# Maximum products of an attention stage in pairs of 64 rows

## The chip, the cores and the metric

The kernel runs on one core of a Trainium2 chip. The time is device time in microseconds (us) from start to end of one execution; the median of several executions counts. Names of the engines as in the profile: PE is TensorE's matmul stream, PEld its weight loads, DVE is VectorE, ACT is ScalarE, POOL is GpSimd, SP issues the DMAs.

## The reference, cut to what matters

One layer of an encoder: 2048 positions, width 1024, float32. Attention has 8 query heads of width 64 on 2 key heads, then comes a gated MLP on chunks, an output projection and a feed-forward part with a convolution. The change lies in the attention alone:

```python
q = rmsnorm(q.reshape(B, S, N_Q_HEADS, HEAD_DIM), g_q[l])
k = rmsnorm(k.reshape(B, S, N_KV_HEADS, HEAD_DIM), g_k[l])
q = apply_axial_rope(q, cos, sin)
k = apply_axial_rope(k, cos, sin)
...
s = jnp.einsum('bqkgd,bskd->bkgqs', qi, k, preferred_element_type=jnp.float32) * scale
p = jax.nn.softmax(s, axis=-1)
return jnp.einsum('bkgqs,bskd->bqkgd', p.astype(v.dtype), v)
```

## The kernel before, in words

Every float32 factor of a matmul is split into a high part and a low part of a narrower type (`h` and `l`), and products are summed from high by high, high by low and low by high. The stages are: projections, attention with the output projection of the block of queries before, the up-projection and the down-projection.

The attention stage works in 32 units: 4 blocks `b` of 512 queries times 8 query heads `hq`. Unit `n` uses these tiles. `K1[i]` holds for key head `i` the 64 rows of the keys' high parts above the 64 rows of their low parts. `K2[i]` holds the high parts again on rows 0 to 63, and a row of -1 on row 64. `X1[n]` holds the queries' high parts twice, on rows 0 to 63 and on rows 64 to 127. `X2[n]` holds the queries' low parts and, on row 64, the maximum of each query's scores. A score tile `st` of 128 keys by 512 queries is the matmul of `K1` with `X1` (L618) plus that of `K2` with `X2` (L619), so the maximum is subtracted by the second matmul. ScalarE then takes the exponential twice (L625 rounded into `ph`, L626 in place), VectorE forms the low part `pl` (L627), and TensorE multiplies `ph` (L607) and `pl` (L613) with the values.

The maximum of unit `n` is found ahead of its scores, by `max_piece`: 16 products per unit, each of 128 queries by 512 keys, with the queries as weights (L538). Each product is reduced by VectorE into a column of `mx` (L539). `max_finish` reduces the columns, transposes them on TensorE (L547) and sends the row to `X2` by DMA. The loop over a unit's 16 key tiles `kt` calls one step of `attend` and one `max_piece`, six steps ahead of the unit that uses it. Scores and products take their PSUM banks from one pool, `ps_s`, with four buffers. Units 0 and, in part, 1 have their products before the loop, in the projection stage (28 products, through `pieces`).

Between these, the loop calls steps of a filler: in the first block the gated MLP, from then on the output projection of the block before, in threes of matmuls (L121, L124, L125). The written order is not the final one: a scheduler that goes by its own timeline of the engines lays out each engine's instructions, subject to data and buffers.

Of the kernel before, what the change touches and what calls it, by code (L numbers as in the profile page):

```python
# [8 lines left out]
F32 = mybir.dt.float32  # L9
F32R = mybir.dt.float32r  # L10
AF = mybir.ActivationFunctionType
ALU = mybir.AluOpType
AX = mybir.AxisListType
# [3 lines left out]
P = 128  # L17
# [6 lines left out]
HD = 64  # L24
QB = 512
NB = S // QB
TPB = QB // P
# [10 lines left out]
PRE1, PRE2 = 7, 12  # L38
# [15 lines left out]
def tile_encoder_layer(  # L54
# [15 lines left out]
    nc = tc.nc  # L70
# [21 lines left out]
    kh_d = dram.tile([P, S], F32, name="kh_d")  # L92
    kl_d = dram.tile([P, S], F32, name="kl_d")
# [396 lines left out]
    kv = pk.enter_context(tc.tile_pool(name="kv", bufs=1, side="right"))  # L490
    VW = 2 * HD + 2
    K1, K2, V = {}, {}, {}

    def alloc_kv(i, pool):
        K1[i] = pool.tile([P, S], F32R, name=f"K1_{i}", bufs=1)
        K2[i] = pool.tile([HD + 1, S], F32R, name=f"K2_{i}", bufs=1)
        V[i] = pool.tile([P, NT, VW], F32R, name=f"V{i}", bufs=1)
        nc.gpsimd.tensor_scalar(
            out=K2[i][HD:HD + 1, :].rearrange("p (a q) -> p a q", q=P),
            in0=ones[HD:HD + 1, :].unsqueeze(1).broadcast_to([1, NT, P]),  # L500
            scalar1=-1.0, scalar2=None, op0=ALU.mult)
        nc.gpsimd.tensor_copy(out=V[i][:, :, 2 * HD:VW],
                              in_=ones[:, 0:2 * NT].rearrange("p (t c) -> p t c", c=2))

    def load_k(i, lo, hi):
        hd, ks = slice(i * HD, (i + 1) * HD), slice(lo, hi)
        nc.sync.dma_start(out=K1[i][0:HD, ks].bitcast(F32), in_=kh_d[hd, ks])
        nc.sync.dma_start(out=K1[i][HD:P, ks].bitcast(F32), in_=kl_d[hd, ks])

    def load_rest(i):  # L510
        nc.sync.dma_start(out=K2[i][0:HD, :].bitcast(F32), in_=kh_d[i * HD:(i + 1) * HD, :])
        nc.sync.dma_start(out=V[i][:, :, 0:2 * HD].bitcast(F32), in_=v_d[:, :, i, :])

    units = [(b, hq) for b in range(NB) for hq in range(NH)]
    NU = len(units)
    X1, X2, mx, attn, q_loads, max_loads = {}, {}, {}, {}, {}, {}

    def load_q(n):
        if n >= NU:
            return  # L520
        b, hq = units[n]
        rows_ = slice((hq % 2) * HD, (hq % 2 + 1) * HD)
        pool = kv if n % 3 < 2 else at
        X1[n] = pool.tile([P, QB], F32R, name=f"X1_{n}", tag=f"X1_{n % 3}", bufs=1)
        X2[n] = pool.tile([HD + 1, QB], F32R, name=f"X2_{n}", tag=f"X2_{n % 3}", bufs=1)
        nc.sync.dma_start(out=X1[n][0:HD, :].bitcast(F32), in_=qh_d[b][rows_, hq // 2, :])
        nc.sync.dma_start(out=X1[n][HD:P, :].bitcast(F32), in_=qh_d[b][rows_, hq // 2, :])
        q_loads[n] = nc.sync.dma_start(out=X2[n][0:HD, :].bitcast(F32), in_=ql_d[b][rows_, hq // 2, :])

    def max_piece(n, p, pool=None, tag="s"):  # L530
        if n >= NU:
            return
        i = units[n][1] // 4
        a, c = divmod(p, 4)
        if n not in mx:
            mx[n] = kv.tile([P, TPB, 4], F32, name="mx", bufs=2)
        s = (pool or ps_s).tile([P, 512], F32, name="sp", tag=tag)
        nc.tensor.matmul(s, lhsT=X1[n][:, a * P:(a + 1) * P], rhs=K1[i][:, c * 512:(c + 1) * 512], start=True, stop=True)  # L538
        nc.vector.tensor_reduce(out=mx[n][:, a, c:c + 1], in_=s, axis=AX.X, op=ALU.max)  # L539

    def max_finish(n):
        if n >= NU:
            return
        mc = kv.tile([P, TPB], F32, name="mc", bufs=2)
        nc.vector.tensor_reduce(out=mc, in_=mx[n], axis=AX.X, op=ALU.max)
        tp = ps_m.tile([P, 512], F32, name="tpm1", tag="m")
        nc.tensor.transpose(out=tp[0:TPB, 0:P], in_=mc, identity=ident)  # L547
        mrow = kv.tile([TPB, P], F32R, name="mrow", bufs=2)
        nc.scalar.copy(out=mrow, in_=tp[0:TPB, 0:P])
        max_loads[n] = nc.sync.dma_start(  # L550
            out=X2[n][HD:HD + 1, :].bitcast(F32).rearrange("o (a q) -> o a q", q=P), in_=mrow.bitcast(F32))

    def pieces(n, todo, banks):
        todo = iter(todo)

        def hook():
            p = next(todo, None)
            if p is not None:
                max_piece(n, p, *banks[p % len(banks)])

        return hook

    for _ in background:
        pass
    alloc_kv(0, kv)
    load_k(0, 0, S - QB)
    load_q(0)
    load_q(1)
# [4 lines left out]
    for k in range(4):  # L573
        z_tile((NSB - 2) * TPH + k, (H, Hn)[k // TPH], hooks[k])
        if k == 1:
            for p in last_chunk:
                max_piece(0, p, *banks[p // 4 % 2])
            max_finish(0)
        if k == 0:
            qk_transposes(*ready.pop(0))  # L580
            load_k(0, S - QB, S)
            load_rest(0)
# [7 lines left out]
    ps_s = pat.enter_context(tc.tile_pool(name="ps_s", bufs=4, space=PSUM))  # L590
# [211 lines left out]
    for n, (b, hq) in enumerate(units):  # L802
        load_q(n + 2)
        if b > 0 and hq == 1:
            filler, due, steps = out_proj(b - 1), 0.0, 86
        cur = attend(n)
        for kt in range(NT):
            next(cur, None)
            if prev is not None:
                next(prev, None)  # L810
            if n == 0 and PRE2 + kt <= NT:
                if PRE2 + kt == NT:
                    max_finish(1)
                else:
                    max_piece(1, PRE2 + kt)
            if n > 0 or kt >= NT - AHEAD:
                ahead, piece = divmod(kt + AHEAD, NT)
                max_piece(n + 1 + ahead, piece)
                if piece == NT - 1:
                    max_finish(n + 1 + ahead)  # L820
            if n > 0:
                due += steps / ((6.6 if b < NB - 1 else 7.25) * NT)
            while due >= 1.0:
                next(filler, None)
                due -= 1.0
        if n == 0:
            alloc_kv(1, at)
            load_k(1, 0, S)
            load_rest(1)
        prev = cur  # L830
        if hq == NH - 1 and b < NB - 1:
            for _ in filler:
                pass
# [155 lines left out]
    for hf in range(NHALF):  # L989
# [5 lines left out]
        for j in (range(NJ - 1, -1, -1) if hf else range(NJ)):  # L995
# [38 lines left out]
            n = HALF + 1 if hf else HALF - 1  # L1034
# [253 lines left out]
def _build(arrays):  # L1288
    import concourse.bacc as bacc

    nc = bacc.Bacc("TRN2", target_bir_lowering=False, num_devices=1)
    args = [nc.dram_tensor(k, v.shape, mybir.dt.from_np(v.dtype), kind="ExternalInput").ap() for k, v in arrays.items()]
    args.append(nc.dram_tensor("out_0_dram", (S, D), F32, kind="ExternalOutput").ap())
    with tile.TileContext(nc, schedule_with_timeline_sim=True) as tc:
        tile_encoder_layer(tc, *args)
    return nc
# [9 lines left out]
```

## Time and profile before

| | us |
|---|---|
| median of 3 runs | 2630.11 |
| lowest and highest | 2629.36, 2635.66 |
| the profiled execution's own time | 2627.74 |
| its span, first to last instruction | 2625.9 |
| TensorE busy in the span | 2549.9 (97%) |
| VectorE busy in the span | 2023.6 (77%) |
| attention stage, from the first maximum product to the last score | 387 to 1263 |

The profiled execution is one run; a term worked out from it is added to its own time. Records of matmuls overlap, since the next one starts while the last still drains: the distance between two starts tells what a matmul costs in a full stream, and the length of its record doesn't.

### The profile page before, as it was taken

Reading aid. Unit: us, or ns where it says so; the run is one execution under the profiler, and the core shown is the slowest. Engines: PE = TensorE matmul, PEld = TensorE weight load, DVE = VectorE, ACT = ScalarE, POOL = GpSimd, SP = SyncE. Lnnn points to the kernel's source line nnn. Section 1 sums busy time; section 2 is a strip of 40 time slices with the busy share of each in tenths; the row PEclk is TensorE's granted clock in tenths of the full one; section 3 lists DMA queues with packets and bytes.
Section 4 is the critical chain, followed back from the end, with each engine's and each line's share of the span. In section 5 each row is a group of like instructions: output and inputs, shape, how many; then the busy total and the mean of one; then the engine's idle time right before and its main releaser. Section 6 shows DMA issues by size and latency. Waiting matters only on the chain.

```text
span 2625.9 us, 34836 instructions
## 1 busy us (share of the span) xinstructions
PE 2549.9 (97%) x11440; PEld 2022.1 (77%) x11440; DVE 2023.6 (77%) x2700; ACT 1440.2 (55%) x2568; POOL 1580.4 (60%) x1280
## 2 busy tenths in 40 slices
PE   7899999999999999999899999999999999999998
PEld 6678776777777777677678888888888888887887
DVE  5776676999888888987568878787576777596796
ACT  3443425788878787877664444464444443323433
POOL 0576757889777777877658788844334551143241
PEclk9999999999999999999999999999999999999999
DMA  8566375451111111111564444554434547977682
GB/s 285 189 205 227 125 201 174 186 196 39 51 49 53 35 58 50 41 41 43 198 215 166 154 164 166 200 189 127 127 120 136 189 149 257 398 279 268 234 294 89
DMA packets 223958, 417.82 MB, mean 159 GB/s; under 512 B 23584, under 2 KB 70432, under 8 KB 220448
## 3 DMA queue, kind: packets, MB, share of 16 engines
q1 hardware_dynamic: 223776, 415.59, 46.9%
q8 instruction: 90, 1.47, 0.2%
q14 instruction: 92, 0.75, 0.1%
HBM read 295.64 MB, written 119.80 MB: 158 GB/s over the span
## 4 chain that ended last, share of the span: by engine, by line
PE 66%; ACT 5%; issue 5%; DVE 5%; DMA 2%; POOL 1%; SPq 0%; POOLq 0%; ACTq 0%; DVEq 0%
PE Y L1013 13%; PE y L1231 9%; PE X L1013 9%; PE Z L1013 9%; PE st L618 4%; PE o L607 4%; PE o L613 4%; PE st L619 4%; PE sp L538 3%; PE po L121 2%; PE po L125 2%; PE po L124 2%; ACT ph L625 1%; ACT st L626 1%; ACT xe L777 1%
## 5 line engine op out<-in xcount | busy, mean ns | idle before, releaser
L631 POOL TENSOR_TENSOR acc<-acc,ph 128x512 f32<-128x512 f32 x416 | 536.8, 1290 | 116.2 <-ACT ph L625 100.8
L625 ACT ACTIVATE ph<-st 128x512 fp32r<-128x512 f32 x512 | 308.8, 603 | 155.3 <-PE st L619 137.7
L870 POOL TENSOR_TENSOR wul<-wuraw,wuh 128x512 fp32r<-128x512 f32 x172 | 273.3, 1592 | 199.5 <-ACT wuh L869 199.1
L539 DVE TENSOR_REDUCE mx<-sp 128x1 f32<-128x512 f32 x512 | 347.3, 684 | 58.1 <-PE sp L538 53.6
L869 ACT CAST wuh<-wuraw 128x512 fp32r<-128x512 f32 x301 | 185.9, 620 | 359.4 <-PE Y L1013 120.3
L627 DVE TENSOR_TENSOR pl<-st,ph 128x512 fp32r<-128x512 f32 x480 | 326.4, 683 | 49.7 <-ACT st L626 44.8
L1044 DVE SCALAR_TENSOR_TENSOR y<-z,vec,y 128x1023 f32<-128x1023 f32 (+1 forms) x176 | 293.5, 1678 | 43.0 <-ACT y L1041 40.1
L626 ACT ACTIVATE st<-st 128x512 f32<-128x512 f32 x480 | 288.9, 602 | 0.0
L1231 PE MATMUL y<-wdh,gh 128*128 128x512 f32 x616 | 238.6, 391 | 3.2 <-DVE c L1181 3.2
L1231 PE MATMUL y<-wdl,gh 128*128 128x512 f32 x616 | 240.2, 390 | 0.0
L1231 PE MATMUL y<-wdh,gl 128*128 128x512 f32 x616 | 238.0, 390 | 0.0
L618 PE MATMUL st<-X,K 128*128 128x512 f32 x512 | 209.6, 409 | 2.9 <-DVE mx L539 1.6
L607 PE MATMUL o<-ph,V 128*128 128x512 f32 x512 | 207.3, 410 | 4.8 <-ACT ph L625 3.0
L1013 PE MATMUL Y<-Fh,wuh 128*128 128x512 f32 x528 | 207.3, 394 | 0.9 <-DVE x L756 0.8
L1013 PE MATMUL Y<-Fl,wuh 128*128 128x512 f32 x528 | 207.9, 394 | 0.0
L1013 PE MATMUL Y<-Fh,wul 128*128 128x512 f32 x528 | 207.6, 393 | 0.0
L538 PE MATMUL sp<-K,X 128*128 128x512 f32 x512 | 204.4, 402 | 3.2 <-DVE mx L539 1.6
L619 PE MATMUL st<-X,K 65*128 65x512 f32 x512 | 202.6, 397 | 0.6 <-DMA X<-mrow 0.6
L613 PE MATMUL o<-pl,V 128*66 128x512 f32 x512 | 201.2, 401 | 1.4 <-DVE acc L647 0.6
L1017 DVE TENSOR_TENSOR z<-Y,z 128x512 f32<-128x512 f32 x132 | 90.2, 685 | 114.6 <-PE Y L1013 114.4
L869 ACT CAST gh<-araw 128x1024 fp32r<-128x1024 f32 x77 | 80.8, 1051 | 156.2 <-PE y L1231 85.3
L959 POOL TENSOR_TENSOR wuraw<-wuraw 128x512 f32<-128x512 f32 x88 | 147.3, 1677 | 22.7 <-DVE wul L870 6.8
(244 smaller groups left out, 6460.0 us busy)
## 6 DMA issues: line engine op xcount, KB each, us to landing
wuraw<-in_w_up_dram SPq DMA_DIRECT2D x151, 256.0 KB
araw<-g_d SPq DMA_DIRECT2D x72, 512.0 KB
wt_d<-wuraw SPq DMA_DIRECT2D x88, 256.0 KB
araw<-gs_d SPq DMA_DIRECT2D x44, 512.0 KB
wuraw<-wt_d SPq DMA_DIRECT2D x84, 256.0 KB
bwa<-in_w_ada_dram SPq DMA_DIRECT2D x64, 256.0 KB
brawx<-in_w_down_dram SPq DMA_DIRECT2D x58, 256.0 KB
hr<-xn_d SPq DMA_DIRECT2D x52, 256.0 KB
```

The costliest lines, as they stand in the source:

```text
L539: nc.vector.tensor_reduce(out=mx[n][:, a, c:c + 1], in_=s, axis=AX.X, op=ALU.max)
L607: nc.tensor.matmul(o1, lhsT=V[i][:, kt, 0:2 * HD], rhs=ph, start=kt == 0, stop=kt == NT - 1)
L613: nc.tensor.matmul(o2[0:HD + 2, :], lhsT=V[i][:, kt, HD:VW], rhs=pl, start=first, stop=kt == NT - 1)
L618: nc.tensor.matmul(s, lhsT=K1[i][:, kc], rhs=X1[n], start=True, stop=False)
L619: scores.append(nc.tensor.matmul(s, lhsT=K2[i][:, kc], rhs=X2[n], start=False, stop=True))
L625: nc.scalar.activation(out=ph, in_=s, func=AF.Exp, scale=SCALE)
L626: exps.append(nc.scalar.activation(out=p, in_=s, func=AF.Exp, scale=SCALE))
L627: eng.tensor_tensor(out=pl, in0=p, in1=ph.bitcast(F32), op=ALU.subtract)
L631: nc.gpsimd.tensor_tensor(out=acc, in0=part, in1=ph.bitcast(F32), op=ALU.add)
L1013: nc.tensor.matmul(acc, lhsT=a[:, k, :], rhs=bb, start=first and k == 0 and n == 0, stop=last and k == KH - 1 and n == 2, skip_group_check ...
L1044: nc.vector.scalar_tensor_tensor(out=y[:, 0:n], in0=z[:, o + tap:o + tap + n], scalar=w[tap], in1=y[:, 0:n], op0=ALU.mult, op1=ALU.add)
L1231: nc.tensor.matmul(ys[tt], lhsT=a[:, ts], rhs=w, start=kt == 0 and n == 0, stop=kt == JH - 1 and n == 2)
```

## The change

Two edits. In `load_k` the halves of `K1` change places: the low parts now lie on rows 0 to 63 and the high parts on rows 64 to 127. The scores of L618 sum over all 128 rows, and `X1` holds the same queries in both halves, so they stay the same sums. The new `max_pair` takes the place of two `max_piece` calls inside the attention loop: for two neighbouring chunks of 512 keys it makes one product on rows 64 to 127 (`X1` and `K1`) and one on rows 0 to 63 (`X1` and `K2`), each into a bank of its own, and reduces both. Each product now sums over 64 rows, the high parts of the keys alone; the low parts of the keys are left out of the maximum. It is called at each second step. The 28 products ahead of the loop keep `max_piece`.

```diff
     def load_k(i, lo, hi):
         hd, ks = slice(i * HD, (i + 1) * HD), slice(lo, hi)
-        nc.sync.dma_start(out=K1[i][0:HD, ks].bitcast(F32), in_=kh_d[hd, ks])
-        nc.sync.dma_start(out=K1[i][HD:P, ks].bitcast(F32), in_=kl_d[hd, ks])
+        nc.sync.dma_start(out=K1[i][HD:P, ks].bitcast(F32), in_=kh_d[hd, ks])
+        nc.sync.dma_start(out=K1[i][0:HD, ks].bitcast(F32), in_=kl_d[hd, ks])
...
+    def max_pair(n, p):
+        if n >= NU:
+            return
+        i = units[n][1] // 4
+        a, c = divmod(p, 4)
+        if n not in mx:
+            mx[n] = kv.tile([P, TPB, 4], F32, name="mx", bufs=2)
+        two = [ps_s.tile([P, 512], F32, name="sp", tag="s") for _ in range(2)]
+        ac = slice(a * P, (a + 1) * P)
+        for k, (s, keys, r) in enumerate(zip(two, (K1[i], K2[i]), (slice(HD, P), slice(0, HD)))):
+            nc.tensor.matmul(s, lhsT=X1[n][r, ac], rhs=keys[r, (c + k) * 512:(c + k + 1) * 512], start=True, stop=True)
+        for k, s in enumerate(two):
+            nc.vector.tensor_reduce(out=mx[n][:, a, c + k:c + k + 1], in_=s, axis=AX.X, op=ALU.max)
...
             if n == 0 and PRE2 + kt <= NT:
                 if PRE2 + kt == NT:
                     max_finish(1)
-                else:
-                    max_piece(1, PRE2 + kt)
+                elif kt % 2 == 0:
+                    max_pair(1, PRE2 + kt)
             if n > 0 or kt >= NT - AHEAD:
                 ahead, piece = divmod(kt + AHEAD, NT)
-                max_piece(n + 1 + ahead, piece)
+                if piece % 2 == 0:
+                    max_pair(n + 1 + ahead, piece)
```

The lines behind it move: in the kernel after, the products of the pairs are L551 and their reductions L553, the scores L632 and L633, the value products L621 and L627, the low part `pl` L641.

How the change moves instructions. TensorE in unit 12 (`X1_12`) at its last key tiles, where the products of unit 14 are made (`X1_14`); `K1_1` and `K2_1` are the tiles of the second key head. Before:

```order
L538 MATMUL sp_7756<-K1_1_4177,X1_14_7502 128x512
L607 MATMUL o1_7507<-ph_7734,V1_4179 128x512
L613 MATMUL o2_7508<-pl_7717,V1_4179 66x512
L618 MATMUL st_7762<-X1_12_6834,K1_1_4177 128x512
L619 MATMUL st_7762<-X2_12_6835,K2_1_4178 128x512
L121 MATMUL po_7709<-wOh7_5962,mh_7436 128x512
L124 MATMUL po_7709<-wOl7_5963,mh_7436 128x512
L125 MATMUL po_7709<-wOh7_5962,ml_7437 128x512
L613 MATMUL o2_7508<-pl_7735,V1_4179 66x512
L538 MATMUL sp_7773<-K1_1_4177,X1_14_7502 128x512
```

The same place after:

```order
L551 MATMUL sp_7756<-K1_1_4177,X1_14_7502 128x512
L621 MATMUL o1_7507<-ph_7737,V1_4179 128x512
L627 MATMUL o2_7508<-pl_7717,V1_4179 66x512
L551 MATMUL sp_7757<-K2_1_4178,X1_14_7502 128x512
L632 MATMUL st_7765<-X1_12_6834,K1_1_4177 128x512
L633 MATMUL st_7765<-X2_12_6835,K2_1_4178 128x512
L627 MATMUL o2_7508<-pl_7738,V1_4179 66x512
L121 MATMUL po_7709<-wOh7_5965,mh_7439 128x512
L124 MATMUL po_7709<-wOl7_5966,mh_7439 128x512
L125 MATMUL po_7709<-wOh7_5965,ml_7440 128x512
```

Two value products on 128 rows now stand between the two members of the pair, and the second product stands three matmuls behind the first instead of nine.

TensorE a unit later (unit 14 scores, products of unit 15), in the kernel after:

```order
L627 MATMUL o2_7819<-pl_8122,V1_4179 66x512
L551 MATMUL sp_8175<-K1_1_4177,X1_15_7813 128x512
L551 MATMUL sp_8176<-K2_1_4178,X1_15_7813 128x512
L621 MATMUL o1_7818<-ph_8141,V1_4179 128x512
L627 MATMUL o2_7819<-pl_8142,V1_4179 66x512
```

Here the two members of a pair follow each other with nothing between them.

VectorE at the first place, before:

```order
L539 TENSOR_REDUCE mx_7724<-sp_7756 128x1
L627 TENSOR_TENSOR pl_7749<-st_7745,ph_7748 128x512
L539 TENSOR_REDUCE mx_7724<-sp_7773 128x1
L627 TENSOR_TENSOR pl_7766<-st_7762,ph_7765 128x512
L539 TENSOR_REDUCE mx_7724<-sp_7790 128x1
```

The same place after:

```order
L553 TENSOR_REDUCE mx_7724<-sp_7725 128x1
L553 TENSOR_REDUCE mx_7724<-sp_7726 128x1
L641 TENSOR_TENSOR pl_7717<-st_7713,ph_7716 128x512
L641 TENSOR_TENSOR pl_7738<-st_7734,ph_7737 128x512
L553 TENSOR_REDUCE mx_7724<-sp_7756 128x1
L641 TENSOR_TENSOR pl_7749<-st_7745,ph_7748 128x512
L553 TENSOR_REDUCE mx_7724<-sp_7757 128x1
```

The reductions of a pair stand in a row in one case, with a low part between them in the next.

## Rows read from the trace of the kernel before

**Rows 1.** The page: engines' busy time in the span; granted clock by slices.
```profile
PE 2549.9 (97%) x11440; PEld 2022.1 (77%) x11440; DVE 2023.6 (77%) x2700; ACT 1440.2 (55%) x2568; POOL 1580.4 (60%) x1280
...
PEclk9999999999999999999999999999999999999999
```

**Rows 2.** Busy time in stretches: stretch, its length, us busy by engine, clock, DMA.
```profile
core 0: us, PE busy (x) PEld busy (x) DVE busy (x) ACT busy (x) POOL busy (x), PEclk, DMA share, GB/s
390.00:1270.00 880.00, 864.36 (x3895) 639.65 (x3894) 751.41 (x1274) 679.22 (x1361) 688.41 (x605) 1.00 0.24 79
...
600.00:1200.00 600.00, 591.45 (x2637) 434.44 (x2636) 523.05 (x880) 478.75 (x965) 463.22 (x420) 1.00 0.15 46
```

**Rows 3.** TensorE's timeline at 901 us: start, record's length, line, matmul, weights, moving.
```profile
901.73 0.40 PE L538 MATMUL sp<-K,X 128*128 128x512 f32 x1
901.96 0.39 PE L618 MATMUL st<-X,K 128*128 128x512 f32 x1
902.20 0.40 PE L619 MATMUL st<-X,K 65*128 65x512 f32 x1
902.43 0.40 PE L121 MATMUL po<-wOh,mh 128*128 128x512 f32 x1
902.66 0.39 PE L124 MATMUL po<-wOl,mh 128*128 128x512 f32 x1
902.90 0.40 PE L125 MATMUL po<-wOh,ml 128*128 128x512 f32 x1
903.13 0.27 PE L547 MATMUL tpm<-ident,mc 128*4 128x128 f32 x1
903.16 0.48 PE L607 MATMUL o<-ph,V 128*128 128x512 f32 x1
903.48 0.40 PE L613 MATMUL o<-pl,V 128*66 128x512 f32 x1
```

**Rows 4.** Groups by line, 600 to 1200 us: count, busy us, mean ns, idle before.
```profile
L539 DVE TENSOR_REDUCE mx<-sp 128x1 f32<-128x512 f32 x354 | 241.4, 684 | 38.3 <-PE sp L538 34.9
...
L618 PE MATMUL st<-X,K 128*128 128x512 f32 x355 | 146.6, 413 | 2.1 <-DVE mx L539 1.1 <-DVE pl L627 0.9
L607 PE MATMUL o<-ph,V 128*128 128x512 f32 x354 | 143.4, 410 | 2.5 <-ACT ph L625 1.0 <-DVE mx L539 1.0
L538 PE MATMUL sp<-K,X 128*128 128x512 f32 x354 | 141.8, 401 | 1.1 <-DVE mx L539 0.6
L613 PE MATMUL o<-pl,V 128*66 128x512 f32 x354 | 141.3, 402 | 1.3 <-DVE acc L647 0.6
L619 PE MATMUL st<-X,K 65*128 65x512 f32 x354 | 140.2, 396 | 0.0
L121 PE MATMUL po<-wOh,mh 128*128 128x512 f32 x167 | 67.1, 402 | 0.0
```

**Rows 5.** Waits, 600 to 1200 us: matmuls, then weight loads; us, times, longest.
```profile
PE st L618 <- DVE mx L539: 1.1, 3, 0.5
...
PEld st L618 <- DVE mx L539: 15.3, 60, 0.8
```

**Rows 6.** TensorE's timeline at 528 us, with four transposes of full shape.
```profile
528.08 0.40 PE L619 MATMUL st<-X,K 65*128 65x512 f32 x1
528.32 0.60 PE L654 MATMUL of<-ident,os 128*128 128x128 f32 x4
528.68 0.48 PE L607 MATMUL o<-ph,V 128*128 128x512 f32 x1
529.00 0.39 PE L613 MATMUL o<-pl,V 128*66 128x512 f32 x1
```

**Rows 7.** SP's timeline at 425 us: loads of the second key head.
```profile
425.46 0.60 SPq L507 DMA_DIRECT2D K<-kh_d  x1
426.11 0.59 SPq L508 DMA_DIRECT2D K<-kl_d  x1
426.75 0.59 SPq L511 DMA_DIRECT2D K<-kh_d  x1
```

## The prediction

> **What bounds the kernel now.** I read the page first. TensorE is busy 97% of the span, with a granted clock of nine tenths or more in every slice [rows 1]. The change touches only the attention stage, so next come the stretches: from 390 to 1270 us, and its even middle from 600 to 1200 us, TensorE is busy 98 to 99% of the time, VectorE 85 to 87%, ScalarE and GpSimd about 77 to 80%; the granted clock there is 1.00, the upper of its two levels (2.4 GHz), so the clock has nothing to give [rows 2]. Busy records of TensorE overlap, so I check that 99% against the spacing of matmuls. In the steady piece at 901 us one 512-column matmul starts every 0.234 us (901.73 to 902.90 in five steps) whatever it computes, on 128 rows or, for L619, on 65; a record is 0.39 to 0.40 us long, so a matmul's last 0.16 us lie under the next one [rows 3]. Then I count the middle stretch [rows 4]: five kinds of some 354 (the two score products L618 and L619, the value products L607 and L613, the maximum products L538) and three of 167 (the output projection) make 2271 matmuls, times 0.234 is 531 us. The other 366 of the 2637 are short, 0.11 us each by the group of four transposes in [rows 6]: 40 us. That is 571 of 600 us, so TensorE is the bound and some 29 us (5%) are holes. Of those, only a few us are waits that the trace names, the largest 1.1 us on the reductions of L539 [rows 5]. A matmul time saved or added here moves the end one for one.
>
> **What the change does to the stream, part by part.** The first 28 maximum products stay as they are. The other 484 become 242 pairs, each product on 64 rows: the first on rows 64 to 127 of the key tile K1, the second on rows 0 to 63 of K2. The number of matmuls, of columns and of reductions stays: each product still streams 512 columns, and its reduction still reads 512 columns at 0.684 us [rows 4].
>
> *The gain.* Two such products can share one streaming time only if they stand next to each other on TensorE. The order of the changed kernel says how often they do: of 242 pairs 34 are adjacent, 108 have one full-height matmul between them, 79 two, 21 three or more. The scheduler places the pair's members apart, as the order pieces in the change show. A product with a 128-row matmul on either side has nobody to share with. So the gain is bounded by 34 x 0.234 = 8.0 us, and its other end is nothing, since no row shows two matmuls running side by side: the nearest, L618 followed by L619, are 0.234 us apart like all others [rows 3]. I take the full 8.0, since nothing else in the array lies on the other half's rows. The Trainium skill (TensorE: Matmul & The Clock Gate, Part 3) states that matmuls on different row groups run concurrently, starting some 4 ns apart; no run here shows that yet. By it the adjacent pairs would save the 8.0 us, without it none; the sum keeps both ends.
>
> *The price of going from 128 rows to 64 and back.* Each adjacent pair is one visit to the half-height shape, each separated pair two: 34 + 2 x 208 = 450 visits. No row of before shows a half-height matmul. The nearest is a visit to a narrow shape: the transpose of the row maxima L547, built on a 128 x 32 part of the array, with four weight columns. From the start of the full matmul before it (902.90) to the start of the second full one behind it (903.48) pass 0.58 us [rows 3]. The work in that is two full matmuls and a 128-column one, 0.234 + 0.11 + 0.234 = 0.578. With four full-shape transposes in its place the same stretch takes 528.08 to 529.00 = 0.92 us, and 0.234 + 4 x 0.11 + 0.234 is 0.908 [rows 6]. So the visit costs 0.00 to 0.01 us; I take 0.01, and 450 x 0.01 = 4.5 us. The other bound is a TensorE that empties at every change of shape: what then shows is the 0.16 us that now lie under the next matmul, twice a visit, 0.32 us x 450 = 144 us. A cost below nothing I exclude, since the columns stay.
>
> The Trainium skill (TensorEngine Tiling (Array Packing), Tiling Modes) states that a change of tiling mode drains TensorE. By that rule each visit is dear and the change loses; the L547 row, which is a change of mode by columns and back, shows no drain. Rows of 64 may differ from columns of 32, so the rule stays as a rival below.
>
> *Banks and VectorE.* Scores and maximum products share four PSUM banks. Their demand now comes as score, product, product, score, and VectorE often reduces twice in a row. In the middle stretch a score's weight load waited 60 times, 15.3 us in all, at most 0.8 us, for a reduction that frees its bank [rows 5]. Nearly all of that is hidden: the matmul itself waited 1.1 us. From the two orders, the last product in a bank and the score that takes the bank next stand a median of 9 matmuls apart before and 10 after, in the nearest tenth 6 before and 4 after. I take nothing, with ends of 9 us gained (a third of the 29 us of holes) and 60 us lost: if each of the 60 loads waited one reduction longer, 60 x 0.684 = 41 us in 600, times 880/600 for the whole stage.
>
> *At nothing:* the swapped halves of K1 are the same two DMAs of the same size on the same SP queue, and the scores sum over both halves, so their place is free. The pairs also read K2, but the first score of a unit on that key head reads all of K2 as well; for the second key head that load is issued at 426.75 us [rows 7], at the stage's start, two units ahead of its first pair. The reduction of the maxima, its transpose and the row's DMA to X2 stay where they were.
>
> **Sum.** -8.0 + 4.5 + 0 = -3.5 us. The profiled execution took 2627.7 us (span 2625.9), 2.4 us under the median of 2630.1; against that median the sum gives 2626.6, so I forecast **2627 us, no change**. About 0.3% (7.9 us) is what a measurement of this kernel can tell from no change; the adjacent pairs alone would just reach it.
>
> **Rivals.**
> 1. *TensorE empties at each change of height* (slower). One visit costs more than 0.035 us from where the loss is over 0.3%: (7.9 + 8.0)/450. With one exposed end per visit, 0.16 us: 450 x 0.16 - 8 = +64 us, 2694. With both, +136 us, 2766. A quarter of an exposed end, 0.04 us at each of two changes: 450 x 0.08 - 8 = +28, 2658. For it: 416 of 484 products are alone among full-height ones, and the stage has no room on TensorE. Against: the L547 visit is free. Chance 0.32, over half of it below 2694.
> 2. *Banks come free later* (slower). The second reduction of a pair is late by up to 0.684 us and the following score's matmul starves; it decides once the waits of L618's matmul grow from 1 us to over 10. Up to +60 us, 2690; more likely a third of it, 2650. Against: distances between bank users barely moved. Chance 0.10.
> 3. *The order itself gets better, or half-height products cost nothing at all* (faster). With free visits the pairs give -8.0, and the new order fills a third of the holes, -9: 2613. Chance 0.15.
> 4. *The pairs work as meant*, all 242 sharing one time: 242 x 0.234 = 56.6 us, 2573. VectorE would allow it: its 523 us in the middle stretch [rows 2] fit in 600 - 41. Against: the order, in which 208 pairs have a full matmul between them. Chance 0.03. That the change doesn't do what it says is thus my main case, not a rival.
>
> **How the numbers follow.** The forecast, within 0.3%, has 0.40 and a range of its own from 2619 to 2637. Slower has 0.32 + 0.10 = 0.42, spread over a long stretch, faster 0.15 + 0.03 = 0.18. The range that should hold the time 8 times in 10 leaves out the all-pairs case and the lowest end of rival 3 (0.06 together) and the upper part of rival 1 (0.13): 2612 to 2700.
>
> **What would show it.** In the profile after, L551 and what follows it: if each half-height matmul and its follower start 0.23 us apart, the visit is free; if 0.3 to 0.4, rival 1 holds, and its cost times 450 must be the loss. In an adjacent pair the second member must start within some hundredths of a us of the first; at 0.23 the gain isn't there either. If the waits of L632 on L553 grow to tens of us, rival 2 holds. The count of matmuls in the stage stays some 3895 [rows 2]. I am wrong if the stage from 390 to 1270 us changes by over 8 us, and above all if separated pairs turn out to cost less than two full matmuls.

## The result, and the profile after

The changed kernel takes 2765.65 us (median of 4 runs, 2762.89 to 2768.12) beside 2629.74 us for the kernel before (4 runs): ratio 1.0515, 95% interval 1.0502 to 1.0527. It is 136 us slower. The forecast was no change at 2627 us with a range up to 2700 us, so the time lies outside.

The page of the kernel after, the lines that answer to [rows 1], and the group of the new products (busy us, mean ns of a record, idle before):

```profile
PE 2694.9 (98%) x11440; PEld 2006.3 (73%) x11440; DVE 2028.8 (73%) x2700; ACT 1443.5 (52%) x2568; POOL 1595.4 (58%) x1280
...
PEclk9899999999999999999999999999999999999999
...
L551 PE MATMUL sp<-K,X 64*128 64x512 f32 x484 | 224.6, 497 | 0.9 <-DVE mx L553 0.9
```

TensorE has the same 11440 matmuls and 145 us more busy time; VectorE's work and the clock have hardly moved. A record of the half-height product is 0.497 us long, where L538 in [rows 4] had 0.401. The stretches of [rows 2], asked of the kernel after:

```profile
core 0: us, PE busy (x) PEld busy (x) DVE busy (x) ACT busy (x) POOL busy (x), PEclk, DMA share, GB/s
390.00:1270.00 880.00, 874.22 (x3354) 533.56 (x3352) 668.51 (x1116) 580.94 (x1154) 592.32 (x518) 0.99 0.21 72
...
600.00:1200.00 600.00, 597.85 (x2277) 359.98 (x2276) 461.26 (x766) 419.33 (x842) 404.16 (x365) 1.00 0.16 52
```

In 600 us TensorE now gets 2277 matmuls done instead of 2637, at the same clock of 1.00 and busy 597.85 us. All other engines have become idler. From the first maximum product to the start of the last score, the stage went from 876 us (387.06 to 1263.23) to 1013 us (387.71 to 1401.03): 137 us, the whole of the loss.

Where it goes shows in the distances of starts. TensorE's timeline at 901 us, the place and form of [rows 3] (start, record's length, line, matmul):

```profile
901.43 0.40 PE L633 MATMUL st<-X,K 65*128 65x512 f32 x1
901.76 0.49 PE L551 MATMUL sp<-K,X 64*128 64x512 f32 x1
902.19 0.44 PE L627 MATMUL o<-pl,V 128*66 128x512 f32 x1
902.56 0.50 PE L551 MATMUL sp<-K,X 64*128 64x512 f32 x1
902.99 0.50 PE L621 MATMUL o<-ph,V 128*128 128x512 f32 x1
903.33 0.39 PE L632 MATMUL st<-X,K 128*128 128x512 f32 x1
903.56 0.40 PE L633 MATMUL st<-X,K 65*128 65x512 f32 x1
```

These are the two members of one pair with a value product between them. A half-height product starts 0.33 us after the full one ahead of it instead of 0.23, and its follower starts 0.43 us later. Where the follower has the second half-height product behind it, that one comes 0.37 us later; where a full one stands there, it comes 0.34 us later (902.99 to 903.33). Only then is the distance 0.23 again. An adjacent pair, at 967 us:

```profile
967.38 0.40 PE L627 MATMUL o<-pl,V 128*66 128x512 f32 x1
967.71 0.50 PE L551 MATMUL sp<-K,X 64*128 64x512 f32 x2
968.26 0.44 PE L627 MATMUL o<-pl,V 128*66 128x512 f32 x1
968.54 0.39 PE L632 MATMUL st<-X,K 128*128 128x512 f32 x1
```

Both members (x2) lie in one record of 0.50 us, the length of a single one: they do run side by side. But there are long distances around the pair too. At this place the 0.55 us behind it hold some 0.12 us in which L627 waited for its low part from VectorE; over all 34 adjacent pairs the medians are 0.33 us ahead, 0.43 behind and 0.34 to the next. The waits on banks, which answer to [rows 5], have not grown (matmuls, then weight loads; us, times, longest):

```profile
PE st L632 <- DVE mx L553: 0.6, 2, 0.3
...
PEld sp L551 <- issue: 68.0, 194, 0.4
...
PEld st L632 <- DVE mx L553: 12.0, 42, 0.6
```

What has grown is the idle time of the weight loads of L551, 68 us in 600, in which they waited for nothing that the profile can name. Two loads beside each other show it, that of the adjacent pair above and that of the full-height L633 at 903 us (weight loads, to be held against the matmuls above):

```profile
967.70 0.19 PEld L551 LDWEIGHTS sp<-K,X 64*128 64x128 f32 x2 [0.42 <-issue]
...
903.33 0.19 PEld L633 LDWEIGHTS st<-X,K 65*128 65x128 f32 x1
```

The first begins 0.01 us before its matmul, after 0.42 us of nothing. The second begins 0.23 us before its own (903.56), under the matmul ahead of it.

### The profile page after: what moved, and what is told of

It reads as the page before. It is cut to its first block, busy times and chain, and to the rows that moved or that the text cites. A ratio compares the mean times of both kernels' runs of the same rounds, so it can differ in the third digit from the quotient of the medians.

```text
span 2763.5 us, 34826 instructions
## 1 busy us (share of the span) xinstructions
PE 2694.9 (98%) x11440; PEld 2006.3 (73%) x11440; DVE 2028.8 (73%) x2700; ACT 1443.5 (52%) x2568; POOL 1595.4 (58%) x1280
## 4 chain that ended last, share of the span: by engine, by line
PE 73%; issue 5%; DVE 5%; POOL 4%; DMA 4%; ACT 2%; SPq 0%; POOLq 0%; DVEq 0%; ACTq 0%
PE Y L1028 12%; PE Z L1028 8%; PE X L1028 8%; PE y L1246 8%; PE sp L551 7%; PE o L621 6%; PE st L632 5%; PE o L627 4%; PE st L633 4%; PE po L125 2%; PE po L121 2%; PE po L124 2%; POOL araw L1118 1%; DMA brawx<-in_w_down_dram 1%; POOL r L110 1%
## 5 line engine op out<-in xcount | busy, mean ns | idle before, releaser
L553 DVE TENSOR_REDUCE mx<-sp 128x1 f32<-128x512 f32 x484 | 329.0, 687 | 125.7 <-PE sp L551 120.5
L885 POOL TENSOR_TENSOR wul<-wuraw,wuh 128x512 fp32r<-128x512 f32 x172 | 283.7, 1652 | 202.3 <-ACT wuh L884 201.5
L641 DVE TENSOR_TENSOR pl<-st,ph 128x512 fp32r<-128x512 f32 x480 | 326.4, 684 | 86.2 <-ACT st L640 80.9
L621 PE MATMUL o<-ph,V 128*128 128x512 f32 x512 | 228.0, 454 | 1.7 <-ACT ph L639 1.3
L551 PE MATMUL sp<-K,X 64*128 64x512 f32 x484 | 224.6, 497 | 0.9 <-DVE mx L553 0.9
L632 PE MATMUL st<-X,K 128*128 128x512 f32 x512 | 215.3, 420 | 2.4 <-DVE mx L553 1.4
L627 PE MATMUL o<-pl,V 128*66 128x512 f32 x512 | 204.5, 409 | 1.4 <-DVE acc L661 0.8
L633 PE MATMUL st<-X,K 65*128 65x512 f32 x512 | 203.6, 398 | 0.0
L551 PEld LDWEIGHTS sp<-K,X 64*128 64x128 f32 x484 | 83.0, 183 | 157.1 <-issue 105.7
```

The costliest lines, as they stand in the source:

```text
L551: nc.tensor.matmul(s, lhsT=X1[n][r, ac], rhs=keys[r, (c + k) * 512:(c + k + 1) * 512], start=True, stop=True)
L553: nc.vector.tensor_reduce(out=mx[n][:, a, c + k:c + k + 1], in_=s, axis=AX.X, op=ALU.max)
L621: nc.tensor.matmul(o1, lhsT=V[i][:, kt, 0:2 * HD], rhs=ph, start=kt == 0, stop=kt == NT - 1)
L627: nc.tensor.matmul(o2[0:HD + 2, :], lhsT=V[i][:, kt, HD:VW], rhs=pl, start=first, stop=kt == NT - 1)
L632: nc.tensor.matmul(s, lhsT=K1[i][:, kc], rhs=X1[n], start=True, stop=False)
L633: scores.append(nc.tensor.matmul(s, lhsT=K2[i][:, kc], rhs=X2[n], start=False, stop=True))
```

## The experiments

Theory A: each passage from full height to 64 rows and back has a price, whatever stands around it. Theory B: the pairs' order, their bursts on VectorE and the shared banks are the cause. The runs of the kernel before beside the first four experiments have a median of 2634.41 us (8 runs, 2629.17 to 2637.0).

**rows65: one row more.** The banks stay, and so does TensorE's order: in the two traces the stage has the same 3885 matmuls, by line and tile names, one after the other. A product of 65 rows no longer fits half of the array.

```diff
-        for k, (s, keys, r) in enumerate(zip(two, (K1[i], K2[i]), (slice(HD, P), slice(0, HD)))):
-            nc.tensor.matmul(s, lhsT=X1[n][r, ac], rhs=keys[r, (c + k) * 512:(c + k + 1) * 512], start=True, stop=True)
+        for k, s in enumerate(two):
+            nc.tensor.matmul(s, lhsT=X1[n][0:HD + 1, ac], rhs=K2[i][:, (c + k) * 512:(c + k + 1) * 512], start=True, stop=True)
```

> The changed kernel with its pairs, its order on TensorE and its banks, but every pair product on 65 rows (rows 0 to 64 of K2 and X1) instead of 64: one row more, and the product no longer counts as half-height. The maximum then carries a number per query that isn't the maximum's, which the softmax cancels. Theory A (each passage from full height to 64 rows and back costs some 0.30 us, whatever else changed): the 450 visits are gone and with them 450 x 0.30 = 135 us, so 2630 us, at most 10 more for the new order. Theory B (the pairs' order, their bursts on VectorE and the shared banks cost the time): nothing of that is changed here, so some 2760 us.

Measured: 2646.28 us, ratio 1.0041 (1.0026 to 1.0055). One row more takes away 119 of the 136 us. TensorE's timeline around a product:

```profile
901.04 0.40 PE L627 MATMUL o<-pl,V 128*66 128x512 f32 x1
901.28 0.40 PE L551 MATMUL sp<-K,X 65*128 65x512 f32 x1
901.51 0.39 PE L621 MATMUL o<-ph,V 128*128 128x512 f32 x1
```

The distances are 0.24 and 0.23 us, as everywhere. Theory B explains at most the 12 us that stay.

**half_single: the price without the pairs.** The kernel before, its order almost kept, with each product of the loop on 64 rows and the halves of `K1` swapped as in the change.

```diff
-        s = (pool or ps_s).tile([P, 512], F32, name="sp", tag=tag)
-        nc.tensor.matmul(s, lhsT=X1[n][:, a * P:(a + 1) * P], rhs=K1[i][:, c * 512:(c + 1) * 512], start=True, stop=True)
+        s, r = (pool or ps_s).tile([P, 512], F32, name="sp", tag=tag), slice(0 if pool else HD, P)
+        nc.tensor.matmul(s, lhsT=X1[n][r, a * P:(a + 1) * P], rhs=K1[i][r, c * 512:(c + 1) * 512], start=True, stop=True)
```

> The kernel before with its loop and almost its order, one product at a time, but the 484 products in the loop are on rows 64 to 127 alone (high parts of the keys, halves of K1 swapped). No pairs. Theory A: 484 visits x 0.30 = +145 us, so some 2775 us, with full-height neighbours starting 0.33 us before and 0.43 us after each. Theory B (pairs, order and banks): nothing of these is here, so some 2630 us.

Measured: 2792.6 us, ratio 1.0599 (1.0583 to 1.0615): 158 us over the kernel before, 0.33 us for each of the 484 products. Its timeline:

```profile
902.01 0.40 PE L125 MATMUL po<-wOh,ml 128*128 128x512 f32 x1
902.34 0.49 PE L538 MATMUL sp<-K,X 64*128 64x512 f32 x1
902.76 0.50 PE L607 MATMUL o<-ph,V 128*128 128x512 f32 x1
903.10 0.27 PE L656 MATMUL ofs<-ident,acc 128*128 128x128 f32 x1
```

The same 0.33, 0.42 and 0.34. Half the rows are enough for the whole loss; pairs, order and banks aren't needed for it.

**pairs_together and together_full: all pairs adjacent.** Both members get one tile of two banks and a higher priority in the scheduler, and the scores have the other two banks; all 242 pairs then stand together. together_full is the same with full-height products.

```diff
-        two = [ps_s.tile([P, 512], F32, name="sp", tag="s") for _ in range(2)]
+        both = ps_s.tile([P, 2, 512], F32, name="sp", tag="pp", bufs=1)
+        two = [both[:, k] for k in range(2)]
...
+        with tc.high_priority():
...
-            s = ps_s.tile([P, 512], F32, name="st", tag="s")
+            s = ps_s.tile([P, 512], F32, name="st", tag="s", bufs=2)
```

> The changed kernel with both members of a pair in one tile of two banks and put on TensorE together: all 242 pairs are adjacent, 242 visits instead of 450; the scores have the other two banks. Theory A: 242 x (0.30 - 0.234) = +16 us over the same kernel with full-height pairs (together_full), if the second member rides free. If a visit's price were per product and not per visit, 484 x 0.30 = +145 us over it. If adjacent members don't overlap, +73 us.

> As pairs_together, but both products of a pair on all 128 rows of K1 and X1, so no visit and nothing that could overlap. It shows what two banks for scores and two for pairs cost by themselves. Theory A: 2630 to 2660 us, all of the excess in waits for banks. Theory B: 2700 us and more, since bursts and banks are the cause.

Measured: pairs_together 2738.43 us (ratio 1.041, 1.0385 to 1.0434), together_full 2722.44 us (1.0332, 1.0317 to 1.0348). The difference is 16.0 us, what Theory A gave: a visit costs more than the product that the pair saves, even if every pair is adjacent. The 88 us of together_full over the kernel before were expected as 30 at most. They are the price of both edits, two of the four banks tied to the pairs and the pairs' priority; how the edits share it wasn't tried. So pairs can't be had together for nothing in this way. Waits named for TensorE make up only part of these 88 us, the largest 21.9 us on the exponentials and 20.9 us of the pairs on the load of their queries, a wait that the kernel before doesn't have; the rest isn't settled.

```profile
PE o L623 <- ACT ph L641: 21.9, 47, 1.8
PE sp L553 <- DMA X<-qh_d: 20.9, 18, 3.4
```

**trains: the price alone.** The kernel before, with trains of extra matmuls of the same operands at the end of the attention stage, in a fixed order; nothing of the computation is left out, and nobody reads their sums. It ran once (2683.74 us), and only the distances in its trace are used. One train of them:

```diff
+    for k in range(8):
+        keep(nc.tensor.matmul(bank[k % 2], lhsT=xx[0:P, 0:P], rhs=kx[0:P, 0:512], start=True, stop=True))
+        keep(nc.tensor.matmul(bank[2 + k % 2], lhsT=xx[0:HD, 0:P], rhs=kx[0:HD, 0:512], start=True, stop=True))
```

> The kernel before, with trains of extra 512-column matmuls of the same operands put at the end of the attention stage, in a fixed order, their sums read by nobody: 16 of full height; 16 on rows 0 to 63; 8 of full height; 8 pairs of rows 64 to 127 and 0 to 63; then 8 times each a full-height one followed by: one on 64 rows, a pair, two pairs, one on 65 rows, one with 32 weight columns, one with 64 weight columns, one on 32 rows; 8 of full height. It measures the price alone, from the distances of starts in the trace. Theory A: 0.234 us within a run of one shape; a pair in a run takes 0.234 in all; full plus one on 64 rows 0.234 x 2 + 0.30 = 0.77 a cycle; full plus a pair 0.77; full plus two pairs 1.0; 65 rows 0.47; 32 weight columns 0.47, as the narrow transpose was free; 64 weight columns 0.47 or 0.77, open; 32 rows 0.77. A rival, that 64 rows themselves are slow, gives 0.4 to 0.5 a matmul in the run of 16 too.

TensorE's timeline, all of these lines at a granted clock of 1.00 (2.4 GHz): a run on 64 rows; pairs in a run; full and half by turns; full and a pair; full and two pairs; 65 rows; 32 and 64 weight columns; 32 rows.

```profile
1280.14 3.99 PE L847 MATMUL tr<-K,X 64*128 64x512 f32 x16
1284.06 0.73 PE L849 MATMUL tr<-K,X 128*128 128x512 f32 x2
...
1286.69 0.39 PE L851 MATMUL tr<-K,X 64*128 64x512 f32 x1
1286.70 0.39 PE L852 MATMUL tr<-K,X 64*128 64x512 f32 x1
1286.93 0.39 PE L851 MATMUL tr<-K,X 64*128 64x512 f32 x1
...
1288.19 0.50 PE L854 MATMUL tr<-K,X 128*128 128x512 f32 x1
1288.62 0.50 PE L855 MATMUL tr<-K,X 64*128 64x512 f32 x1
1289.05 0.50 PE L854 MATMUL tr<-K,X 128*128 128x512 f32 x1
...
1295.01 0.50 PE L857 MATMUL tr<-K,X 128*128 128x512 f32 x1
1295.44 0.50 PE L858 MATMUL tr<-K,X 64*128 64x512 f32 x1
1295.45 0.49 PE L859 MATMUL tr<-K,X 64*128 64x512 f32 x1
1295.87 0.51 PE L857 MATMUL tr<-K,X 128*128 128x512 f32 x1
...
1303.02 0.49 PE L861 MATMUL tr<-K,X 128*128 128x512 f32 x1
...
1304.11 0.49 PE L861 MATMUL tr<-K,X 128*128 128x512 f32 x1
...
1311.67 0.40 PE L867 MATMUL tr<-K,X 128*128 128x512 f32 x1
1311.91 0.40 PE L868 MATMUL tr<-K,X 65*128 65x512 f32 x1
1312.14 0.40 PE L867 MATMUL tr<-K,X 128*128 128x512 f32 x1
...
1314.97 0.40 PE L870 MATMUL tr<-K,X 128*128 128x512 f32 x1
1315.21 0.39 PE L871 MATMUL tr<-K,X 128*32 128x512 f32 x1
1315.44 0.40 PE L870 MATMUL tr<-K,X 128*128 128x512 f32 x1
...
1318.46 0.40 PE L874 MATMUL tr<-K,X 128*64 128x512 f32 x1
1318.69 0.40 PE L873 MATMUL tr<-K,X 128*128 128x512 f32 x1
...
1322.70 0.50 PE L876 MATMUL tr<-K,X 128*128 128x512 f32 x1
1323.13 0.49 PE L877 MATMUL tr<-K,X 32*128 32x512 f32 x1
1323.55 0.50 PE L876 MATMUL tr<-K,X 128*128 128x512 f32 x1
```

| cycle | measured, us | at 0.234 a streaming | price of the visit |
|---|---|---|---|
| run on 64 rows, each (1280.14 to 1284.06 in 16, with the change at its end) | 0.245 | 0.234 | none within the run |
| pair in a run, both | 0.23 to 0.24 | 0.234 | none |
| full, one on 64 rows | 0.85 | 0.468 | 0.38 |
| full, a pair | 0.86 | 0.468 | 0.39 |
| full, two pairs | 1.09 | 0.702 | 0.39 |
| full, 65 rows | 0.47 | 0.468 | 0 |
| full, 32 or 64 weight columns | 0.46 to 0.47 | 0.468 | 0 |
| full, one on 32 rows | 0.85 | 0.468 | 0.38 |

The rows by themselves aren't slow, the second member of a pair starts 0.00 to 0.01 us after the first and is free, and fewer weight columns are free. A change of height costs some 0.195 us, and a visit has two of them. The 0.39 us of a visit are more than the 0.30 expected from the kernel after, and 0.39 is also what the timeline of the kernel after shows around a lone product: 0.33 + 0.43 + 0.34 - 3 x 0.234 = 0.40.

The cycles on 32 rows are read up to 1325.25 us. Soon after, still in this train, the granted clock fell to its lower level (1.2 GHz), and a cycle took 1.44 us:

```profile
1326.00:1331.00 5.00, 5.00 (x8) 2.13 (x8) 0.00 (x0) 0.00 (x0) 0.00 (x0) 0.50 0.00 0
```

In the 22 us from 1288 to 1310 us, with 64 rows by turns with full height, it stayed at 1.00.

**The price in each kernel.** The stage's length less its streaming time (3278 matmuls of 512 columns x 0.234, 96 of 256 columns x 0.125, 510 short ones x 0.115; 838 us in all) is what TensorE lost:

| kernel | stage, us | lost, us | visits |
|---|---|---|---|
| before | 876.2 | 38 | 0 |
| rows65 | 890.9 | 53 | 0 |
| after | 1013.3 | 176 | 450 |
| half_single | 1038.1 | 200 | 484 |

From rows65 to after, the visits cost 1013.3 - 890.9 + 8.0 (saved by 34 pairs) = 130 us net, 0.29 each; in half_single (1038.1 - 876.2)/484 = 0.33. That is less than 0.39, because part of the price falls into time in which TensorE stood idle before. The traces show it, since the order of rows65 and after is the same. I add up, over all matmuls of the stage, the distances of starts less the streaming times. At the 450 places (the distances into a visit, within it, out of it and the next one) after has lost 165 us, or 173 with the 8.0 that the pairs save: 0.38 a visit, as in the trains. At the same places rows65 has lost 36 us, and everywhere else 17 us against 11 in after. So a visit pays the full price on average, and some 42 us of the 173 lie where rows65 had holes.

No version that beats the kernel before came in sight: a pair saves 0.234 us and a visit costs 0.29 to 0.39. Two pairs in a visit save 0.08 us against five full matmuls (1.09 to 1.17), at 120 visits some 10 us (an estimate from the table), and need all four banks at once, where tying two of them, with the pairs' priority, cost 88 us. It wasn't tried.

## Why the prediction was wrong

- *What bounds the kernel*: right. TensorE's lost time moved the end one for one, 137 us of stage for 136 us of time.
- *The gain*: right, and small as read from the order: 34 adjacent pairs, each sharing one streaming time, 8.0 us. The side-by-side start that no row of before showed is there (0.00 to 0.01 us apart).
- *The price of the visit*: this step failed. I took 0.01 us from the nearest row, the narrow transpose L547 in [rows 3], and measured are 0.39 us in a dense stream and 0.29 net in this kernel, 130 us instead of 4.5. The row was read rightly (32 and 64 weight columns are free in the trains too), but it was a change by columns, and a change by rows behaves differently. The other end of that bound, both ends of a matmul's 0.16 us exposed, 0.32 us a visit, gave 2766 us as rival 1's upper case, the time that was measured. That it fits so well is luck: the price itself is 0.39, part of it fell into holes, and the 12 us of the next item came on top. I put only 0.13 of the chance above 2700 us. The Trainium skill (TensorEngine Tiling (Array Packing), Tiling Modes) states that a change of tiling mode drains TensorE. A price at each change of rows agrees, 0.195 us; whether TensorE empties in it no record shows, and fewer weight columns had no price.
- *Banks and VectorE*: taken at nothing; measured with rows65 at 12 us (1.0041), just over what can be told from no change, and with no wait that stands out. Mis-sized by a little, in the direction of rival 2.
- *Sum with the measured terms*: -8 + 130 + 12 = +134, against +136 measured. This is no independent test, since the 130 come from the same stages; what stands by itself is the 0.38 a visit counted from the starts and the 0.39 of the trains.
- *The signs given in advance*: the distances of 0.3 to 0.4 us around L551 were named as the sign of rival 1, and they are there. "Its cost times 450 must be the loss" holds only with the net price, since some 42 of the 173 us fall into holes.

## What to carry to other kernels

Before splitting a matmul over row halves of the array, count the passages between full and half height in the final order of the instructions, not the pairs in the source: here each passage there and back cost 0.39 us in a dense stream, more than the 0.234 us of a 512-column product, so a lone pair among full-height matmuls loses even when both members run together. Long runs of half-height pairs could pay, if there are banks for them: the 8 pairs of the train took 2.07 us from the first start to the start of the full matmul behind (1286.12 to 1288.19), where 16 full products stream 3.74 us. When a cost has no row in the trace, and the nearest row changes another dimension, keep the far bound as a full case: here it was the nearer one.

## What the runs showed of the hardware

One row decides: 65 rows run as a full-height matmul with neighbours 0.23 us apart, 64 or 32 rows cost 0.195 us at each change. With it goes the weight load's head start: that of the adjacent pair at 967 us began 0.01 us ahead of its matmul, where that of L633 at 903 us had 0.23. A load of 128 weight columns takes 0.19 us (both lines above), about as long as the price of one change. In the kernel after, the load of L627 with its 66 columns takes 0.14 us, and where L627 is the first behind a visit, the full-height matmul behind it starts 0.28 us later (968.26 to 968.54; the median of 34 such places is 0.28 too) instead of 0.34. So the price looks like one weight load that is no longer hidden; that wasn't tried by itself.
